# A row-wise cosine similarity on one core: all loads on one queue, tiles on another address grid, the last block in pieces, and most of the epilogue moved into the loop

## The chip, the cores and the metric

One core of a Trainium2 chip. The metric is the device time of one execution in microseconds (us). The kernel before takes 1268.29 us (median of 5 runs, 1268.15 to 1268.68). The profiled execution of it has a span of 1266.4 us; times in the traces count from its start.

## The reference

```python
# x, y: 8192 x 8192, float32
x_norm = np.linalg.norm(x, axis=1, keepdims=True)
y_norm = np.linalg.norm(y, axis=1, keepdims=True)
return np.sum(x * y, axis=1) / (x_norm.squeeze() * y_norm.squeeze() + 1e-8)
```

Each row needs three sums over 8192 columns: x·y, x·x and y·y. The inputs are 537 MB, the output is 32 KB.

## The kernel before

Rows are taken in 64 blocks of 128, one row in each partition. A block is a 4 MB tile of x and one of y, each 128 x 8192, with two buffers each. DVE (VectorE) multiplies x by y and sums; ACT (ScalarE) squares x and sums, then y. x is loaded through SP's DMA queue, y through ACT's.

```python
    consts = ctx.enter_context(tc.tile_pool(name="consts", bufs=1))
    xyacc = consts.tile([P, M], fp32)      # also xxacc, yyacc, ident: 1280 bytes in all
    # ... (cut)
    for b in range(nblk):
        # ... (cut; K is 1, so F is 8192 and there is one k)
            xt = xpool.tile([P, F], fp32)
            nc.sync.dma_start(out=xt, in_=x[r0 : r0 + P, c0 : c0 + F])
            yt = ypool.tile([P, F], fp32)
            nc.scalar.dma_start(out=yt, in_=y[r0 : r0 + P, c0 : c0 + F])
            prod = spool.tile([P, F], bf16, name="prod")
            nc.vector.tensor_tensor_reduce(out=prod, in0=xt, in1=yt, # ... (cut)
                accum_out=xyacc[:, m : m + 1])
            sqr = spool.tile([P, F], bf16, name="sqr")
            nc.scalar.activation(out=sqr, in_=xt, # Square (cut)
                accum_out=xxacc[:, m : m + 1])
            nc.scalar.activation(out=sqr, in_=yt, # Square (cut)
                accum_out=yyacc[:, m : m + 1])
    # epilogue, 64 columns, once at the end
    nc.vector.tensor_tensor(out=nn, in0=xxs, in1=yys, op=mult)
    nc.scalar.sqrt(out=sq, in_=nn)
    nc.vector.tensor_scalar(out=sqe, in0=sq, scalar1=1e-8, scalar2=None, op0=add)
    nc.vector.reciprocal(out=rcp, in_=sqe)
    nc.vector.tensor_tensor(out=res, in0=xys, in1=rcp, op=mult)
    # ... (cut: PSUM tile)
    nc.tensor.transpose(rest, res, ident)
    nc.vector.tensor_copy(out=ot, in_=rest)
    nc.sync.dma_start(out=out.rearrange("(b p) -> b p", p=P), in_=ot)
```

## Time and profile before

| stretch of the span, us | from | to | long |
|---|---|---|---|
| until the first input data moves | 0 | 1.8 | 1.8 |
| the input stream, to the last landing | 1.8 | 1248.4 | 1246.6 |
| to the end of ACT's last square and its sum | 1248.4 | 1260.1 | 11.8 |
| to the issue of the output store | 1260.1 | 1263.65 | 3.5 |
| to the end | 1263.65 | 1266.37 | 2.72 |

Begin with the question which engine is full. These are lines of the page of the kernel before: two digit rows and the DMA rows, each with 40 equal slices of the span (a digit is the busy share in tenths); then the shares of the chain that ended last, by line; then DVE's group of instructions (busy us, mean ns, idle us before them and what ended most of it).

```profile
span 1266.4 us, 830 instructions
...
DVE  2254453443543534535435345354353453543534
ACT  3777686686776866867768668677686686776776
...
DMA  9999999999999999999999999999999999999993
GB/s 409 436 431 431 431 431 431 431 431 431 432 434 436 431 435 432 431 431 431 431 431 431 431 433 434 434 431 436 431 432 431 431 431 431 431 433 431 437 431 146
...
DMA xt<-in_x_dram 42%; DMA yt<-in_y_dram 42%; DVE prod L55 14%; ACT sqr L72 1%; ACT sqr L66 0%; ACT L100 0%; DVEq L55 0%; DVE rcp L104 0%; SPq L50 0%; ACTq L52 0%; PE rest L111 0%; DVE xyacc L55 0%; ACTq L66 0%; DVE ot L113 0%; ACTq L140 0%
...
L55 DVE CUSTOM_DVE_ANT_0 prod<-xt,yt 128x8192 bf16<-128x8192 f32 x64 | 556.3, 8692 | 700.4 <-DMA yt<-in_y_dram 700.4
...
```

DVE and ACT have gaps in every slice; the DMA engines are at 9 tenths or more in 39 of 40 slices and move about 431 GB/s. DVE waits 700 us for y in all. The slices are coarse (they read 409 to 437 GB/s in the body); the period of a block, below, gives 431.8 GB/s. The last slice, at 146 GB/s, is the tail.

The chain of waits gives the period of a block. Columns: start, duration, what. This chain alternates between the loads of x and y, so it meets DVE once in three blocks.

```profile
...
1037.07 8.69 DVE prod L55
...
1045.83 25.07 DMA xt<-in_x_dram
...
1071.04 24.16 DMA yt<-in_y_dram
...
1095.35 8.69 DVE prod L55
...
1153.64 8.69 DVE prod L55
...
```

From 1037.07 to 1095.35 to 1153.64, three blocks take 58.28 and 58.29 us: 19.43 us a block, for 8.39 MB: 431.8 GB/s.

How long a load takes from issue to landing stands in the page's DMA issues (line, queue, count, KB each, median us):

```profile
...
yt<-in_y_dram ACTq DMA_DIRECT2D x64, 4096.0 KB, 24.2
xt<-in_x_dram SPq DMA_DIRECT2D x64, 4096.0 KB, 25.1
...
```

And the tail, in the timeline (start, duration, engine, line, operation; in brackets the idle time before it and who ended it):

```profile
...
1245.84 7.03 ACT L66 ACTIVATE sqr<-xt 128x8192 bf16<-128x8192 f32 x1 [5.13 <-DMA xt<-in_x_dram]
1248.53 8.69 DVE L55 CUSTOM_DVE_ANT_0 prod<-xt,yt 128x8192 bf16<-128x8192 f32 x1 [8.47 <-DMA yt<-in_y_dram]
...
1253.00 7.03 ACT L72 ACTIVATE sqr<-yt 128x8192 bf16<-128x8192 f32 x1
...
1259.94 0.19 ACT L72 ACTIVATION_READ_ACCUMULATOR sqr<-yt 128x1 f32 x1
1260.14 1.28 ACT L100 ACT_TABLE_LOAD   x1
...
1261.95 0.55 DVE L104 RECIPROCAL rcp<-sqe 128x64 f32<-128x64 f32 x1
...
1263.65 0.55 SPq L114 DMA_DIRECT2D out_dram<-ot  x1
```

The last x lands first and the last y 2.7 us later. ACT needs 14.3 us for both squares and starts only at 1245.84, so it, not DVE, ends the block. Then comes a second table load for Sqrt, of 1.28 us; the square root itself starts right behind it, at 1261.43.

### The profile page before, as it was taken

To read this page: it belongs to the slowest core of one execution; us is meant where nothing else is said; L and a number is where in the kernel's file an instruction comes from. 1 tells how busy PE (TensorE), PEld (TensorE's weight loads), DVE (VectorE), ACT (ScalarE), POOL (GpSimd) and SP (SyncE) were. 2 spreads that over 40 slices of the span, in tenths; PEclk is the share of its full clock that TensorE was granted. 3 is DMA by queue.
4 is the path that set the end of the run, shared out by engine and by line. 5 is a ranking of instruction groups with operands and counts; after the bars stand their busy time and mean duration, and the time that the engine had idled before them with its cause. 6 is when DMAs were issued, how large, how long until landed. Compare 5 with 4: busy or idle time off the path is not lost.

```text
span 1266.4 us, 830 instructions
## 1 busy us (share of the span) xinstructions
PE 0.4 (0%) x1; PEld 0.1 (0%) x1; DVE 558.3 (44%) x133; ACT 914.5 (72%) x259; POOL 0.7 (0%) x6
## 2 busy tenths in 40 slices
PE   0000000000000000000000000000000000000000
PEld 0000000000000000000000000000000000000000
DVE  2254453443543534535435345354353453543534
ACT  3777686686776866867768668677686686776776
POOL 0000000000000000000000000000000000000000
DMA  9999999999999999999999999999999999999993
GB/s 409 436 431 431 431 431 431 431 431 431 432 434 436 431 435 432 431 431 431 431 431 431 431 433 434 434 431 436 431 432 431 431 431 431 431 433 431 437 431 146
DMA packets 18519, 536.97 MB, mean 424 GB/s; under 512 B 2064, under 2 KB 2128, under 8 KB 2128
## 3 DMA queue, kind: packets, MB, share of 16 engines
q1 hardware_dynamic: 9296, 268.47, 49.3%
q10 hardware_dynamic: 9216, 268.44, 49.2%
q14 instruction: 7, 0.06, 0.0%
HBM read 536.87 MB, written 0.03 MB: 424 GB/s over the span
## 4 chain that ended last, share of the span: by engine, by line
DMA 83%; DVE 15%; ACT 1%; issue 1%; ACTq 0%; DVEq 0%; SPq 0%; PE 0%
DMA xt<-in_x_dram 42%; DMA yt<-in_y_dram 42%; DVE prod L55 14%; ACT sqr L72 1%; ACT sqr L66 0%; ACT L100 0%; DVEq L55 0%; DVE rcp L104 0%; SPq L50 0%; ACTq L52 0%; PE rest L111 0%; DVE xyacc L55 0%; ACTq L66 0%; DVE ot L113 0%; ACTq L140 0%
## 5 line engine op out<-in xcount | busy, mean ns | idle before, releaser
L55 DVE CUSTOM_DVE_ANT_0 prod<-xt,yt 128x8192 bf16<-128x8192 f32 x64 | 556.3, 8692 | 700.4 <-DMA yt<-in_y_dram 700.4
L66 ACT ACTIVATE sqr<-xt 128x8192 bf16<-128x8192 f32 x64 | 449.9, 7030 | 342.3 <-DMA xt<-in_x_dram 342.3
L72 ACT ACTIVATE sqr<-yt 128x8192 bf16<-128x8192 f32 x64 | 449.9, 7030 | 3.1 <-DMA yt<-in_y_dram 1.1
L66 ACT ACTIVATION_READ_ACCUMULATOR sqr<-xt 128x1 f32 x64 | 11.9, 187 | 0.0
L72 ACT ACTIVATION_READ_ACCUMULATOR sqr<-yt 128x1 f32 x64 | 11.9, 186 | 0.0
L55 DVE DVE_READ_ACCUMULATOR2_ANT xyacc<- 128x1 f32 x64 | 5.3, 82 | 0.0
L66 ACT ACT_TABLE_LOAD x1 | 1.3, 1283 | 1.7 <-PEq L129 1.7
L98 DVE TENSOR_TENSOR nn<-xxacc,yyacc 128x64 f32<-128x64 f32 x1 | 0.2, 226 | 2.9 <-ACT sqr L72 2.9
L100 ACT ACT_TABLE_LOAD x1 | 1.3, 1283 | 0.0
L102 DVE TENSOR_SCALAR sqe<-sq 128x64 f32<-128x64 f32 x1 | 0.2, 195 | 1.3 <-ACT sq L100 1.3
L111 PE MATMUL rest<-ident,res 128*64 128x128 f32 x1 | 0.4, 393 | 1262.9 <-DVE res L106 1262.9
L104 DVE RECIPROCAL rcp<-sqe 128x64 f32<-128x64 f32 x1 | 0.6, 554 | 0.0
L113 DVE COPY ot<-rest 64x128 f32<-64x128 f32 x1 | 0.3, 282 | 0.6 <-PE rest L111 0.6
masks.py:199 POOL TENSOR_SCALAR_AFFINE_SELECT ident<-ident 128x128 f32<-128x128 f32 x1 | 0.3, 295 | 0.1
L100 ACT ACTIVATE sq<-nn 128x64 f32<-128x64 f32 x1 | 0.3, 256 | 0.0
L111 PEld LDWEIGHTS rest<-ident,res 128*64 128x64 f32 x1 | 0.1, 128 | 1262.9 <-issue 1262.9
L106 DVE TENSOR_TENSOR res<-xyacc,rcp 128x64 f32<-128x64 f32 x1 | 0.2, 225 | 0.0
masks.py:197 POOL MEMSET ident<- 128x128 f32 x1 | 0.2, 205 | 0.3 <-POOLq L129 0.3
L129 POOL MEMSET const-bfloat16-1.0<- 128x1 bf16 x1 | 0.1, 103 | 0.0
L129 POOL MEMSET const-uint8-127<- 128x1 uint8 x1 | 0.1, 102 | 0.0
L129 POOL MEMSET const-float32-0.0<- 128x1 f32 x1 | 0.1, 100 | 0.2 <-issue 0.2
L129 POOL MEMSET const-float32-1.0<- 128x1 f32 x1 | 0.1, 100 | 0.0
## 6 DMA issues: line engine op xcount, KB each, us to landing
yt<-in_y_dram ACTq DMA_DIRECT2D x64, 4096.0 KB, 24.2
xt<-in_x_dram SPq DMA_DIRECT2D x64, 4096.0 KB, 25.1
out_dram<-ot SPq DMA_DIRECT2D x1, 32.0 KB, 1.9
```

What stands on the lines that cost most here:

```text
L55: nc.vector.tensor_tensor_reduce(out=prod, in0=xt, in1=yt, scale=1.0, scalar=0.0, op0=mult, op1=add, accum_out=xyacc[:, m : m + 1],)
L66: nc.scalar.activation(out=sqr, in_=xt, func=mybir.ActivationFunctionType.Square, accum_out=xxacc[:, m : m + 1],)
L72: nc.scalar.activation(out=sqr, in_=yt, func=mybir.ActivationFunctionType.Square, accum_out=yyacc[:, m : m + 1],)
L98: nc.vector.tensor_tensor(out=nn, in0=xxs, in1=yys, op=mult)
L100: nc.scalar.sqrt(out=sq, in_=nn)
L102: nc.vector.tensor_scalar(out=sqe, in0=sq, scalar1=1e-8, scalar2=None, op0=add)
L104: nc.vector.reciprocal(out=rcp, in_=sqe)
L106: nc.vector.tensor_tensor(out=res, in0=xys, in1=rcp, op=mult)
L111: nc.tensor.transpose(rest, res, ident)
L113: nc.vector.tensor_copy(out=ot, in_=rest)
L129: nc = _bacc.Bacc("TRN2", target_bir_lowering=False, num_devices=1)
```

## The change

It has four parts. All loads go to SP's queue. A padding tile moves x and y onto addresses that are multiples of 256 bytes (they were 128 bytes off: the first x tile stood at 17792 and now stands at 18176). The last block is loaded and reduced in pieces of 4096, 2048, 1024 and 1024 columns, so that little work is left after the last landing. And the epilogue of the first 62 blocks runs, and stores, beside the stream, with Sqrt's table set loaded at the start and used for Square as well; the add of 1e-8 is dropped. (The squares of x and of y also get a scratch tile each.) The core of the diff:

```diff
+    nl = nblk - 1
+    ne = nblk - 2
+    ends = [4096, 6144, 7168, 8192]
     # ... (cut: constants)
-    xyacc = consts.tile([P, M], fp32)
-    xxacc = consts.tile([P, M], fp32)
-    yyacc = consts.tile([P, M], fp32)
+    acc = consts.tile([P, 3 * nblk], fp32, name="acc")  # 768 bytes
+    fa = consts.tile([P, 3 * NP], fp32, name="fa")  # 48, takes 64
+    pad = consts.tile([P, 64], fp32, name="pad")  # rows of x and y on the 256-byte grid
     # ... (cut: the other tiles)
-            nc.sync.dma_start(out=xt, in_=x[r0 : r0 + P, c0 : c0 + F])
-            nc.scalar.dma_start(out=yt, in_=y[r0 : r0 + P, c0 : c0 + F])
+        if b < nl:
+            nc.sync.dma_start(out=xt, in_=x[r0 : r0 + P, :])
+            nc.sync.dma_start(out=yt, in_=y[r0 : r0 + P, :])
+            if b == 0:
+                nc.gpsimd.memset(one, 1.0)
+                nc.scalar.sqrt(out=dum, in_=one)  # loads the table set with Sqrt and Square
+                # ... (cut)
+            dve_dot(prod, xt, yt, a0v[:, 2, b : b + 1])
+            act_sq(sqx, xt, a0v[:, 0, b : b + 1])
+            act_sq(sqy, yt, a0v[:, 1, b : b + 1])
+            if b == ne - 1:  # the epilogue of the first 62 blocks
+                # ... (cut: mult, sqrt, reciprocal, mult on 62 columns)
+                nc.tensor.transpose(psE[0:ne, :], res[:, 0:ne], ident)
+                nc.vector.tensor_copy(out=ot[0:ne, :], in_=psE[0:ne, :])
+                nc.gpsimd.dma_start(out=outv[0:ne, :], in_=ot[0:ne, :])
+            continue
+        for k, (s, e) in enumerate(zip(starts, ends)):
+            cs = slice(s, e)
+            nc.sync.dma_start(out=xt[:, cs], in_=x[r0 : r0 + P, cs])
+            nc.sync.dma_start(out=yt[:, cs], in_=y[r0 : r0 + P, cs])
+            dve_dot(prod[:, cs], xt[:, cs], yt[:, cs], fav[:, 2, k : k + 1])
+            act_sq(sqx[:, cs], xt[:, cs], fav[:, 0, k : k + 1])
+            if k == 2:
+                dve_dot(sqy[:, cs], yt[:, cs], yt[:, cs], fav[:, 1, k : k + 1])
+            else:
+                act_sq(sqy[:, cs], yt[:, cs], fav[:, 1, k : k + 1])
+    # the last block's sums join its column; then the epilogue of the last two blocks
+    nc.vector.tensor_reduce(out=a0v[:, :, nl : nl + 1], in_=fav, axis=mybir.AxisListType.X, op=add)
+    nc.vector.tensor_tensor(out=nnL, in0=a0v[:, 0, ne:nblk], in1=a0v[:, 1, ne:nblk], op=mult)
+    nc.scalar.sqrt(out=sqL, in_=nnL)
     # ... (cut: reciprocal, mult, transpose, copy on 2 columns)
+    nc.sync.dma_start(out=outv[ne:nblk, :], in_=otL)
```

More of the change, by code (lines that the diff above doesn't have):

```diff
@@ L20 @@
     fp32 = mybir.dt.float32
+    bf16 = mybir.dt.bfloat16
     N, D = x.shape
@@ L25 @@
     F = D
-    K = D // F
-    M = nblk * K
-    bf16 = mybir.dt.bfloat16
     mult = mybir.AluOpType.mult
     add = mybir.AluOpType.add
+    nl = nblk - 1
+    ne = nblk - 2
+    sq_f = mybir.ActivationFunctionType.Square
+    ends = [4096, 6144, 7168, 8192]
+    starts = [0] + ends[:-1]
+    NP = len(ends)
     consts = ctx.enter_context(tc.tile_pool(name="consts", bufs=1))
-    xyacc = consts.tile([P, M], fp32)
-    xxacc = consts.tile([P, M], fp32)
-    yyacc = consts.tile([P, M], fp32)
+    acc = consts.tile([P, 3 * nblk], fp32, name="acc")
     ident = consts.tile([P, P], fp32)
-    make_identity(nc, ident)
+    fa = consts.tile([P, 3 * NP], fp32, name="fa")
+    one = consts.tile([P, 1], fp32, name="one")
+    dum = consts.tile([P, 1], fp32, name="dum")
+    pad = consts.tile([P, 64], fp32, name="pad")
+    a0v = acc.rearrange("p (g b) -> p g b", g=3)
+    fav = fa.rearrange("p (g k) -> p g k", g=3)
     xpool = ctx.enter_context(tc.tile_pool(name="xp", bufs=2))
@@ L42 @@
     spool = ctx.enter_context(tc.tile_pool(name="scratch", bufs=1))
+    fin = ctx.enter_context(tc.tile_pool(name="fin", bufs=1))
+    nn = fin.tile([P, nblk], fp32)
+    sq = fin.tile([P, nblk], fp32)
+    rcp = fin.tile([P, nblk], fp32)
+    res = fin.tile([P, nblk], fp32)
+    ot = fin.tile([nblk, P], fp32)
+    otL = fin.tile([2, P], fp32, name="otL")
+    nnL = fin.tile([P, 2], fp32, name="nnL")
+    sqL = fin.tile([P, 2], fp32, name="sqL")
+    rcpL = fin.tile([P, 2], fp32, name="rcpL")
@@ new lines, with dve_dot, act_sq @@
+    resL = fin.tile([P, 2], fp32, name="resL")
+    pspool = ctx.enter_context(tc.tile_pool(name="ps", bufs=1, space=bass.MemoryType.PSUM))
+    psE = pspool.tile([nblk, P], fp32, name="psE")
+    psL = pspool.tile([2, P], fp32, name="psL")
+    outv = out.rearrange("(b p) -> b p", p=P)
+    def dve_dot(o, a, b_, accum):
+        nc.vector.tensor_tensor_reduce(
+            out=o, in0=a, in1=b_, scale=1.0, scalar=0.0, op0=mult, op1=add, accum_out=accum
+        )
+    def act_sq(o, a, accum):
+        nc.scalar.activation(out=o, in_=a, func=sq_f, accum_out=accum)
@@ L44 @@
     for b in range(nblk):
         r0 = b * P
-        for k in range(K):
-            c0 = k * F
-            m = b * K + k
-            xt = xpool.tile([P, F], fp32)
-            nc.sync.dma_start(out=xt, in_=x[r0 : r0 + P, c0 : c0 + F])
-            yt = ypool.tile([P, F], fp32)
-            nc.scalar.dma_start(out=yt, in_=y[r0 : r0 + P, c0 : c0 + F])
-            prod = spool.tile([P, F], bf16, name="prod")
-            nc.vector.tensor_tensor_reduce(
-                out=prod,
-                in0=xt,
-                in1=yt,
-                scale=1.0,
-                scalar=0.0,
-                op0=mult,
-                op1=add,
-                accum_out=xyacc[:, m : m + 1],
-            )
-            sqr = spool.tile([P, F], bf16, name="sqr")
-            nc.scalar.activation(
-                out=sqr,
-                in_=xt,
-                func=mybir.ActivationFunctionType.Square,
-                accum_out=xxacc[:, m : m + 1],
-            )
-            nc.scalar.activation(
-                out=sqr,
-                in_=yt,
-                func=mybir.ActivationFunctionType.Square,
-                accum_out=yyacc[:, m : m + 1],
-            )
@@ L79 @@
-    fin = ctx.enter_context(tc.tile_pool(name="fin", bufs=1))
-    if K > 1:
-        ax = mybir.AxisListType.X
-        xys = fin.tile([P, nblk], fp32)
-        xxs = fin.tile([P, nblk], fp32)
-        yys = fin.tile([P, nblk], fp32)
-        nc.vector.tensor_reduce(
-            out=xys, in_=xyacc.rearrange("p (b k) -> p b k", k=K), axis=ax, op=add
-        )
-        nc.vector.tensor_reduce(
-            out=xxs, in_=xxacc.rearrange("p (b k) -> p b k", k=K), axis=ax, op=add
-        )
-        nc.vector.tensor_reduce(
-            out=yys, in_=yyacc.rearrange("p (b k) -> p b k", k=K), axis=ax, op=add
-        )
-    else:
-        xys, xxs, yys = xyacc, xxacc, yyacc
@@ L97 @@
-    nn = fin.tile([P, nblk], fp32)
-    nc.vector.tensor_tensor(out=nn, in0=xxs, in1=yys, op=mult)
-    sq = fin.tile([P, nblk], fp32)
-    nc.scalar.sqrt(out=sq, in_=nn)
-    sqe = fin.tile([P, nblk], fp32)
-    nc.vector.tensor_scalar(out=sqe, in0=sq, scalar1=1e-8, scalar2=None, op0=add)
-    rcp = fin.tile([P, nblk], fp32)
-    nc.vector.reciprocal(out=rcp, in_=sqe)
-    res = fin.tile([P, nblk], fp32)
-    nc.vector.tensor_tensor(out=res, in0=xys, in1=rcp, op=mult)
-    assert nblk <= P
-    pspool = ctx.enter_context(tc.tile_pool(name="ps", bufs=1, space=bass.MemoryType.PSUM))
@@ L110 @@
-    rest = pspool.tile([nblk, P], fp32, name="rest")
-    nc.tensor.transpose(rest, res, ident)
-    ot = fin.tile([nblk, P], fp32)
-    nc.vector.tensor_copy(out=ot, in_=rest)
-    nc.sync.dma_start(out=out.rearrange("(b p) -> b p", p=P), in_=ot)
+        xt = xpool.tile([P, F], fp32)
+        yt = ypool.tile([P, F], fp32)
+        prod = spool.tile([P, F], bf16, name="prod")
+        sqx = spool.tile([P, F], bf16, name="sqx")
+        sqy = spool.tile([P, F], bf16, name="sqy")
+        if b < nl:
[4 more added lines that the diff above has]
+                nc.scalar.sqrt(out=dum, in_=one)
+                nc.gpsimd.memset(pad, 0.0)
+                make_identity(nc, ident)
+            dve_dot(prod, xt, yt, a0v[:, 2, b : b + 1])
+            act_sq(sqx, xt, a0v[:, 0, b : b + 1])
+            act_sq(sqy, yt, a0v[:, 1, b : b + 1])
+            if b == ne - 1:
+                nc.vector.tensor_tensor(
+                    out=nn[:, 0:ne], in0=a0v[:, 0, 0:ne], in1=a0v[:, 1, 0:ne], op=mult
+                )
+                nc.scalar.sqrt(out=sq[:, 0:ne], in_=nn[:, 0:ne])
+                nc.vector.reciprocal(out=rcp[:, 0:ne], in_=sq[:, 0:ne])
+                nc.vector.tensor_tensor(
+                    out=res[:, 0:ne], in0=a0v[:, 2, 0:ne], in1=rcp[:, 0:ne], op=mult
+                )
+                nc.tensor.transpose(psE[0:ne, :], res[:, 0:ne], ident)
+                nc.vector.tensor_copy(out=ot[0:ne, :], in_=psE[0:ne, :])
+                nc.gpsimd.dma_start(out=outv[0:ne, :], in_=ot[0:ne, :])
+            continue
@@ new lines @@
+    nc.vector.tensor_reduce(out=a0v[:, :, nl : nl + 1], in_=fav, axis=mybir.AxisListType.X, op=add)
+    nc.vector.tensor_tensor(out=nnL, in0=a0v[:, 0, ne:nblk], in1=a0v[:, 1, ne:nblk], op=mult)
+    nc.scalar.sqrt(out=sqL, in_=nnL)
+    nc.vector.reciprocal(out=rcpL, in_=sqL)
+    nc.vector.tensor_tensor(out=resL, in0=a0v[:, 2, ne:nblk], in1=rcpL, op=mult)
+    nc.tensor.transpose(psL, resL, ident)
+    nc.vector.tensor_copy(out=otL, in_=psL)
+    nc.sync.dma_start(out=outv[ne:nblk, :], in_=otL)
```

## The prediction

> **What bounds the kernel now.** The input stream. The page's slices show the DMA engines at 9 tenths in 39 of 40 slices and about 431 GB/s; DVE is busy 44%, ACT 72%. In the chain of waits, one block (x and y, 8.39 MB) takes 19.43 us: three blocks per 58.29 us, 1153.6 to 1211.9. That is 431.7 GB/s. [...] The rest of the span is head and tail. By the timeline, the last y lands at 1248.5, and then 17.9 us carry no input: ACT squares x (begun 1245.8) and y, 8192 columns each, until 1260.1; table load 1.28; the 64-column chain to 1263.65; output store to 1266.4.
>
> **What the change does.**
> 1. Last block in pieces of 4096, 2048, 1024, 1024 columns, y's third square on DVE. ACT costs 7.03 us for 8192 columns, 0.26 for 64, plus 0.19 to read the sum, so I estimate 3.8, 2.1 and 1.3 us per piece. ACT is still busy with block 62's y when the pieces begin to land; laying the pieces out in time, ACT ends about 3.5 us after the last landing instead of 11.6. Saved: about 8 us.
> 2. Epilogue of blocks 0 to 61 moved under the stream (DVE waits 10.7 us in every block, so it is free). The last two blocks' epilogue works on 2 columns: no table load (Sqrt and Square share one set, loaded at the start), no add of 1e-8, reciprocal no longer 0.55 us; a small reduction (about 0.2 us) comes in. From ACT's end to the store about 1.8 us instead of 3.5. Saved: about 1.7 us. The store still costs its 2.7 us.
> 3. The x and y tiles move from SBUF addresses 128 bytes off the 256-byte grid (17792, read from the built program) onto it (18176). [...] This is the least certain term.
> 4. All loads on SP's queue instead of SP and ACT: the same engines, so no bandwidth. The queue is refilled with about 10 us of work still in it, so it should not run dry. Landing times should split: x about 20 us, y about 30 us, instead of 25 and 24. A separate scratch for sqy costs nothing.
>
> Nothing else in the body is on the critical path.
>
> **Predicted.** 1268.3 - 8 - 1.7 - 4 = 1254.5 us; range 1249 to 1260. Faster by over 2% (below 1242.9): 0.03; within 2%: 0.96; slower by over 2%: 0.01.
>
> **What would show each step.** (1) timeline: last landing to end of ACT's squares 3 to 4 us. (2) from there to the store's issue about 1.8 us, one table load in all. (3) block period 19.36 us or less; unchanged 19.43 means alignment is worth nothing. (4) median landings of 20 and 30 us, DMA slices without gaps.
>
> **What would make it wrong.** A bubble between transfers on a single queue, which the second queue hid: 0.1 us per transfer would be 13 us over 128. [...] The small 62-row store beside the stream delaying one DMA engine, so that the last piece lands late. ACT's backlog in the last block larger or smaller than laid out.

The sum came to 1254.5 us: 1268.3 less 8 (term 1), 1.7 (term 2) and 4 (term 3).

## The result, and the profile after

The kernel after takes 1251.64 us (median of 7 runs, 1251.49 to 1251.81), against 1268.33 us for the kernel before in the same rounds. The ratio is 0.9868, with a 95% interval of 0.9858 to 0.9878. Ratios here are the mean time of one kernel's fast runs over that of the other's of the same rounds, so not quite the ratio of the medians that are quoted. The results are correct.

| step, us in the two profiles | before | after | saved |
|---|---|---|---|
| start to the last landing of input | 1248.4 | 1244.4 | 4.0 |
| last landing to the end of ACT's last square | 11.8 | 1.8 | 10.0 |
| to the issue of the last store | 3.5 | 1.8 | 1.7 |
| issue of that store to the end | 2.72 | 2.07 | 0.7 |
| span | 1266.4 | 1250.0 | 16.4 |

The last landing is read from the trace's completion records: a load is taken as complete at the last of its 16 reports.

The lines of the page after that answer to those before:

```profile
span 1250.0 us, 929 instructions
...
DMA  9999999999999999999999999999999999999997
GB/s 403 436 436 433 428 431 436 436 435 430 428 435 436 434 435 428 430 436 436 434 434 429 430 436 435 436 431 429 433 436 435 436 428 428 436 436 436 433 428 318
...
DMA yt<-in_y_dram 75%; DVE prod L67 22%; ACT sqy L72 1%; SPq L82 1%; ACT sqx L72 1%; DVEq L67 0%; DVE acc L67 0%; SPq L83 0%; PE psL L121 0%; DVE otL L122 0%; ACT sqL L118 0%; DVE acc L116 0%; DVE rcpL L119 0%; DVE resL L120 0%; DVE nnL L117 0%
...
L86 ACT ACT_TABLE_LOAD x1 | 1.3, 1283 | 0.7 <-PEq L138 0.7
...
```

The last slice now carries 318 GB/s instead of 146: the tail is shorter. There is one table load, of 1283 ns; before there were two of that length. The chain now runs through y alone, since y, issued behind x in the same queue, is the later to land (29.4 us from issue against 20.1, below), and meets DVE once in two blocks:

```profile
...
836.75 8.69 DVE prod L67
...
845.93 29.38 DMA yt<-in_y_dram
...
875.47 8.69 DVE prod L67
...
914.19 8.69 DVE prod L67
...
```

From 836.75 to 875.47 to 914.19, two blocks take 38.72 us: 19.36 us a block instead of 19.43. The landing times split, x at 20.1 us and y, which stands behind it in the queue, at 29.4 us:

```profile
...
xt<-in_x_dram SPq DMA_DIRECT2D x63, 4096.0 KB, 20.1
yt<-in_y_dram SPq DMA_DIRECT2D x63, 4096.0 KB, 29.4
...
```

The tail of the timeline, from the store of the first 62 rows (POOL, 1216.18) on; ACT's and DVE's pieces of the last block between 1231.97 and 1245.03 are left out:

```profile
...
1216.18 0.67 POOL L103 DMA_DIRECT2D out_dram<-ot  x1 [1214.75 <-DVE ot L102]
...
1224.94 7.03 ACT L72 ACTIVATE sqy<-yt 128x8192 bf16<-128x8192 f32 x1 [2.62 <-DMA yt<-in_y_dram]
...
1231.97 3.60 ACT L72 ACTIVATE sqx<-xt 128x4096 bf16<-128x4096 f32 x1
...
1245.03 1.05 ACT L72 ACTIVATE sqy<-yt 128x1024 bf16<-128x1024 f32 x1
...
1245.97 0.19 ACT L72 ACTIVATION_READ_ACCUMULATOR sqy<-yt 128x1 f32 x1
1246.20 0.17 DVE L116 TENSOR_REDUCE acc<-fa 128x3 f32<-128x12 f32 x1 [0.45 <-ACT sqy L72]
...
1246.83 0.17 DVE L119 RECIPROCAL rcpL<-sqL 128x2 f32<-128x2 f32 x1 [0.27 <-ACT sqL L118]
...
1247.96 0.33 SPq L123 DMA_DIRECT2D out_dram<-otL  x1
```

Between 1224.94 and 1245.97 ACT is never idle: the pieces land faster than ACT squares them, and it ends 1.8 us after the last landing at 1244.4.

### The profile page after: what moved, and what is told of

Its sections match the earlier page's. It is cut to its first block, busy times and chain, and to the rows that moved or that the text cites. A ratio compares the mean times of both kernels' runs of the same rounds, so it can differ in the third digit from the quotient of the medians.

```text
span 1250.0 us, 929 instructions
## 1 busy us (share of the span) xinstructions
PE 0.8 (0%) x2; PEld 0.2 (0%) x2; DVE 560.5 (45%) x145; ACT 913.5 (73%) x270; POOL 1.5 (0%) x9
## 4 chain that ended last, share of the span: by engine, by line
DMA 75%; DVE 22%; ACT 1%; SPq 1%; issue 1%; DVEq 0%; PE 0%; ACTq 0%
DMA yt<-in_y_dram 75%; DVE prod L67 22%; ACT sqy L72 1%; SPq L82 1%; ACT sqx L72 1%; DVEq L67 0%; DVE acc L67 0%; SPq L83 0%; PE psL L121 0%; DVE otL L122 0%; ACT sqL L118 0%; DVE acc L116 0%; DVE rcpL L119 0%; DVE resL L120 0%; DVE nnL L117 0%
## 5 line engine op out<-in xcount | busy, mean ns | idle before, releaser
L67 DVE CUSTOM_DVE_ANT_0 prod<-xt,yt 128x8192 bf16<-128x8192 f32 (+2 forms) x67 | 556.8, 8310 | 685.2 <-DMA yt<-in_y_dram 685.1
L72 ACT ACTIVATE sqx<-xt 128x8192 bf16<-128x8192 f32 (+2 forms) x67 | 450.4, 6723 | 168.6 <-DMA xt<-in_x_dram 168.6
L72 ACT ACTIVATE sqy<-yt 128x8192 bf16<-128x8192 f32 (+1 forms) x66 | 449.4, 6810 | 161.7 <-DMA yt<-in_y_dram 161.7
L72 ACT ACTIVATION_READ_ACCUMULATOR sqx<-xt 128x1 f32 x67 | 12.5, 187 | 0.0
L72 ACT ACTIVATION_READ_ACCUMULATOR sqy<-yt 128x1 f32 x66 | 12.3, 187 | 0.0
L67 DVE DVE_READ_ACCUMULATOR2_ANT acc<- 128x1 f32 x63 | 5.2, 82 | 0.0
L86 ACT ACT_TABLE_LOAD x1 | 1.3, 1283 | 0.7 <-PEq L138 0.7
L101 PEld LDWEIGHTS psE<-ident,res 128*62 128x62 f32 x1 | 0.1, 129 | 1215.1 <-issue 1215.1
## 6 DMA issues: line engine op xcount, KB each, us to landing
xt<-in_x_dram SPq DMA_DIRECT2D x63, 4096.0 KB, 20.1
yt<-in_y_dram SPq DMA_DIRECT2D x63, 4096.0 KB, 29.4
```

What stands on the lines that cost most here:

```text
L67: nc.vector.tensor_tensor_reduce(out=o, in0=a, in1=b_, scale=1.0, scalar=0.0, op0=mult, op1=add, accum_out=accum)
L72: nc.scalar.activation(out=o, in_=a, func=sq_f, accum_out=accum)
L86: nc.scalar.sqrt(out=dum, in_=one) # loads the table set with Sqrt and Square
L101: nc.tensor.transpose(psE[0:ne, :], res[:, 0:ne], ident)
```

## The experiments

The prediction was near the measured time. But a sum can be near with wrong terms, and one part of the change (the queue) had been given no value at all. So each part was undone alone in the kernel after, and the two that touch the stream were also done alone in the kernel before.

### Address grid and queue: four corners

Theory A: the stream's 4 us come from the addresses. Theory Q: they come from the single queue. The trace records each DMA packet; a 32 KB packet is one row of one tile, and there are 16384 of them (16128 where the last block is in pieces). Their mean duration measures the stream without the tail.

`b_grid` is the kernel before on the grid:

```diff
     make_identity(nc, ident)
+    pad = consts.tile([P, 32], fp32, name="pad")  # 128 bytes: x and y on the 256-byte grid
+    nc.gpsimd.memset(pad, 0.0)
```

> The kernel before with 128 bytes of padding, so that x and y tiles start on the 256-byte grid; still two queues, tail untouched. Theory A (the offset costs the stream): the mean DMA record of a 32 KB row falls from 1217.6 ns to 1213.7 ns as in the kernel after, the period of a block from 19.42 to 19.36 us, the time by 4 us to 1264.3. Theory Q (two queues cost the stream, the address nothing): rows stay at 1217.6 ns and the time at 1268.3.

`b_one` is the kernel before on one queue:

```diff
-            nc.scalar.dma_start(out=yt, in_=y[r0 : r0 + P, c0 : c0 + F])
+            nc.sync.dma_start(out=yt, in_=y[r0 : r0 + P, c0 : c0 + F])
```

> The kernel before with y's loads moved to SP's queue; tiles still 128 bytes off the grid, tail untouched. Theory A: rows stay near 1217.6 ns; the time stays at 1268.3 or moves by at most about 1 us (the last y lands at nearly the same time, but x earlier, which lets ACT square x before y lands: the tail alone may gain 3 to 4 us, from ACT's 7 us for x ending before the last landing; that is not the stream). Theory Q: rows at 1213.7 ns, and 4 us more off the time.

`a_off` is the kernel after off the grid by 128 bytes:

```diff
-    pad = consts.tile([P, 64], fp32, name="pad")
+    pad = consts.tile([P, 32], fp32, name="pad")
```

> The kernel after with 128 bytes less padding, so that x and y tiles are again 128 bytes off the grid; one queue, all else as after. Theory A: rows back at 1217.6 ns, block period 19.42 us, time 1255.6 (+4). Theory Q: 1213.7 ns and 1251.6.

`a_two` is the kernel after on two queues:

```diff
         if b < nl:
             nc.sync.dma_start(out=xt, in_=x[r0 : r0 + P, :])
-            nc.sync.dma_start(out=yt, in_=y[r0 : r0 + P, :])
+            nc.scalar.dma_start(out=yt, in_=y[r0 : r0 + P, :])
```

> The kernel after with y's loads of the first 63 blocks back on ACT's queue; tiles on the grid, the last block's pieces still on SP. Theory A: rows stay at 1213.7 ns and the time within 1 us of 1251.6, but for what the order of landing does at the end. Theory Q: rows at 1217.6 ns, time 1255.6. Landings of x and y about 25 and 24 us again under both.

Measured, with rounds of its own in which the kernel before took 1268.17 us:

| kernel | grid | queues | mean 32 KB packet, ns | time, us | ratio to before |
|---|---|---|---|---|---|
| before | 128 off | 2 | 1217.6 | 1268.17 | 1 |
| b_grid | on | 2 | 1213.6 | 1263.73 | 0.9965 (0.9953 to 0.9978) |
| b_one | 128 off | 1 | 1217.6 | 1263.99 | 0.9968 (0.9955 to 0.9980) |
| a_off | 128 off | 1 | 1217.7 | 1255.98 | 0.9904 (0.9890 to 0.9917) |
| a_two | on | 2 | 1213.8 | 1254.04 | 0.9889 (0.9874 to 0.9904) |
| after | on | 1 | 1213.7 | 1251.64 (other rounds) | 0.9868 |

The packets follow the address and not the queue, in all four corners: theory A holds and Q falls. The arithmetic closes: 16384 packets over 16 engines are 1024 for each in the mean, and 1024 x 4.0 ns is 4.1 us; the two grid comparisons give 4.4 and 4.3 us. (Over all rounds the kernel before took 1268.17 to 1268.40 us, so times of different rounds can be compared to about 0.2 us.)

Still, the single queue is worth 4.2 us alone in the kernel before and 2.4 us in the kernel after, without a faster packet. It acts in the tail, by the order in which the last loads land. `b_one`, timeline of its tail:

```profile
...
1238.63 7.03 ACT L66 ACTIVATE sqr<-xt 128x8192 bf16<-128x8192 f32 x1 [2.64 <-DMA xt<-in_x_dram]
...
1248.32 7.03 ACT L72 ACTIVATE sqr<-yt 128x8192 bf16<-128x8192 f32 x1 [2.57 <-DMA yt<-in_y_dram]
1248.41 8.69 DVE L55 CUSTOM_DVE_ANT_0 prod<-xt,yt 128x8192 bf16<-128x8192 f32 x1 [10.76 <-DMA yt<-in_y_dram]
...
1255.46 1.28 ACT L100 ACT_TABLE_LOAD   x1
1257.03 0.08 DVE L55 DVE_READ_ACCUMULATOR2_ANT xyacc<- 128x1 f32 x1
...
1259.49 0.55 SPq L114 DMA_DIRECT2D out_dram<-ot  x1
```

The last y lands when it did before (1248.2 against 1248.4). But x landed 9.7 us ahead of it, at 1238.6, so ACT has x squared before y comes and ends at 1255.5 instead of 1260.1. What ends the block is now DVE with its 8.69 us, at 1257.1: 3.0 us earlier than ACT did before. The other 1.1 us of the gain is the second table load, which now runs while DVE still works: from the end of the block to the issue of the store it is 2.4 us instead of 3.5. In `a_two` the same acts one block earlier. Its timeline:

```profile
...
1227.21 7.03 ACT L72 ACTIVATE sqy<-yt 128x8192 bf16<-128x8192 f32 x1 [1.41 <-DMA yt<-in_y_dram]
...
1234.24 3.60 ACT L72 ACTIVATE sqx<-xt 128x4096 bf16<-128x4096 f32 x1
...
1248.25 0.18 ACT L72 ACTIVATION_READ_ACCUMULATOR sqy<-yt 128x1 f32 x1
...
```

Against the kernel after, y of block 62 starts to be squared at 1227.21 instead of 1224.94, since with two queues it lands that much later; ACT then has no gap, and ends 2.3 us later, though the last input lands at almost the same time (1244.5 against 1244.4).

One point of the expectation for `a_two` failed: its median landings were 18.9 us for x and 16.8 us for y, not 25 and 24. No run asked why, or whether the time depends on it.

### The pieces alone undone

`a_whole` (with the padding corrected by 32 bytes, since `fa` shrinks, so that the tiles stay on the grid):

```diff
-    ends = [4096, 6144, 7168, 8192]
+    ends = [8192]
-            if k == 2:
+            if k == 99:
```

> The kernel after with the last block loaded and reduced whole (one piece); grid, one queue and early epilogue kept. If the pieces are worth what the prediction's first term says they are worth by themselves (8 us), 1259.6. My theory now: with one queue x of the last block lands 10 us before y, so ACT is no longer the limit and DVE's 8.69 us after the last landing is; ACT ended 1.8 us after the last landing in the kernel after, so the pieces are worth about 8.8 - 1.8 - 0.4 (small rows cost 0.4 us of stream) = 6.6 us: 1258.2. The rest of the tail's gain came from the queue.

The 0.4 us for small rows are an estimate from the trace after: its packets of 16, 8 and 4 KB took 611, 309 and 159 ns in the mean, 4, 6 and 7 ns over their share of the 1213.7 ns of a 32 KB row, and the mean share of one of 16 engines is 16, 16 and 32 of them.

It took 1258.67 us (before in these rounds: 1268.26 us; ratio 0.9924, 0.9911 to 0.9936). That is 7.0 us above the kernel after. Its timeline:

```profile
...
1234.44 7.03 ACT L72 ACTIVATE sqx<-xt 128x8192 bf16<-128x8192 f32 x1 [2.54 <-DMA xt<-in_x_dram]
...
1244.09 7.03 ACT L72 ACTIVATE sqy<-yt 128x8192 bf16<-128x8192 f32 x1 [2.53 <-DMA yt<-in_y_dram]
1244.17 8.69 DVE L67 CUSTOM_DVE_ANT_0 prod<-xt,yt 128x8192 bf16<-128x8192 f32 x1 [10.64 <-DMA yt<-in_y_dram]
...
1252.97 0.16 DVE L116 TENSOR_REDUCE acc<-fa 128x3 f32<-128x3 f32 x1
...
```

With one queue, ACT has squared x before y lands (the start at 1234.44 leaves 2.5 us of rest), and DVE's 8.69 us from 1244.17 end the block. So the pieces do not take 11.8 us of ACT to 1.8 by themselves. The queue takes ACT out of the way, and the pieces then cut DVE's one long instruction: DVE ended 8.9 us after the last landing here (1244.0 to 1252.9), and the block in the kernel after ends 1.8 us after it. With two queues the pieces cut ACT's work instead: ACT ends 11.9 us after the last landing in `b_grid` (1243.8 to 1255.7) and 4.0 us after it in `a_two` (1244.5 to 1248.4), though these two also differ in the epilogue, and all of the last block in `a_two` comes through one queue.

### The early epilogue undone, and the store beside the stream

`a_epi` puts the whole 64-column epilogue, the second table load, the add of 1e-8 and a single store back at the end:

```diff
-                nc.scalar.sqrt(out=dum, in_=one)  # loads the table set with Sqrt and Square
-            if b == ne - 1:  # the epilogue of the first 62 blocks
-                # ... (cut: all of it)
     nc.vector.tensor_reduce(out=a0v[:, :, nl : nl + 1], in_=fav, axis=mybir.AxisListType.X, op=add)
-    # ... (cut: the 2-column epilogue)
+    nc.vector.tensor_tensor(out=nn, in0=a0v[:, 0, :], in1=a0v[:, 1, :], op=mult)
+    nc.scalar.sqrt(out=sq, in_=nn)
+    nc.vector.tensor_scalar(out=sq, in0=sq, scalar1=1e-8, scalar2=None, op0=add)
+    # ... (cut: reciprocal, mult, transpose, copy)
+    nc.sync.dma_start(out=outv, in_=ot)
```

> The kernel after with the whole epilogue (64 columns, table load for Sqrt, the add of 1e-8, one store of 64 rows) at the end again, nothing stored beside the stream. Theory: ACT's end to the store's issue 1.76 us becomes about 3.6 (0.2 reduction + the 3.5 us of before), the store 2.07 becomes 2.75: 1254.1 to 1254.3. If the store beside the stream had cost the stream anything that counts, it would be up to 0.5 us less than this.

It took 1253.80 us (ratio 0.9885, 0.9870 to 0.9900): 2.2 us above the kernel after, a little under the range expected. From ACT's end to the issue of the store it was 3.5 us in the profile, and the store took 2.74 us. Against that, ACT ended 0.26 us earlier than in the kernel after (1245.90 against 1246.16).

`a_late` keeps the early arithmetic and takes only the store beside the stream away:

```diff
-                nc.tensor.transpose(psE[0:ne, :], res[:, 0:ne], ident)
-                nc.vector.tensor_copy(out=ot[0:ne, :], in_=psE[0:ne, :])
-                nc.gpsimd.dma_start(out=outv[0:ne, :], in_=ot[0:ne, :])
     # ... (cut)
-    nc.tensor.transpose(psL, resL, ident)
-    nc.vector.tensor_copy(out=otL, in_=psL)
-    nc.sync.dma_start(out=outv[ne:nblk, :], in_=otL)
+    nc.tensor.transpose(psE, res, ident)
+    nc.vector.tensor_copy(out=ot, in_=psE)
+    nc.sync.dma_start(out=outv, in_=ot)
```

> The kernel after without the store of 62 rows beside the stream: one transposition, copy and store of all 64 rows at the end; the rest of the early epilogue kept. The landings of block 61 and after spread from 1.62 to 2.15 us where that store ran; theory B (the store delays one DMA engine): the spread stays near 1.6 and the last landing comes 0.4 to 0.5 us earlier. The time: theory C (ACT's backlog of squares, not the landing, ends the last block) gives no gain from that, and the 64-row store costs 0.7 us: 1252.3. If the landing ends the block: 1251.8.

It took 1252.29 us (ratio 0.9874, 0.9860 to 0.9887), the figure of theory C; but the profile shows that C was right for the wrong reason. Without the store, the 16 reports of the last load spread over 1.66 us instead of 2.02, and the last landing came at 1244.04 instead of 1244.38, which looks like theory B. But in the kernel after the spread had already grown, from 1.62 to 2.15 us, in a load that had landed by 1215.12, and the store was only issued at 1216.18. The DMA records show something else just before: a packet of queue 14, which the page calls "instruction" (8 KB, 309 ns, at 1208.98), and behind it one 32 KB row that took 1751 ns instead of 1213. `a_late` has the same pair (at 1209.91, a row of 1746 ns), but there the spread stayed at 1.7 us. The first reports of the last load came at 1242.4 in both. So the difference is no work of the store, and theory B falls: by its size (the spread grew by 0.53 us), the row's 0.54 us fell on the part of the load that reported last already in the kernel after, and not in `a_late`; that is inferred, since the records name no engine. The earlier landing did reach ACT's end, which came 0.35 us earlier, because block 62's y landed earlier too (ACT starts on it at 1224.59 instead of 1224.94), and that is where ACT's unbroken run of squares starts. The gain was then more than paid back: 0.7 us for a store of 64 rows instead of 2 (2.72 against 2.07 us from issue to end) and 0.1 us for the wider transposition. So storing early saves about 0.8 us at the end by the profiles, and 0.65 us by the timed runs; a cost of the store to the stream was not seen.

### Is ACT's backlog the last limit?

`a_best` loads block 62 in two halves as well and the last block in six pieces, so that both engines are further ahead when the last pieces land:

```diff
-    ends = [4096, 6144, 7168, 8192]
+    cut = {nl - 1: [4096, 8192], nl: [2048, 4096, 6144, 7168, 7680, 8192]}
     # ... (cut: one fa for each of the two blocks, padding kept on the grid)
-            if k == 2:
+            if k == 3:
```

> The kernel after with block 62 in two halves and the last block in six pieces (2048, 2048, 2048, 1024, 512, 512), so that ACT and DVE have half of block 62 behind them when its last half lands. Theory C: ACT's end comes 0.9 to 1.2 us after the last landing instead of 1.8; minus about 0.2 us of stream for more small rows: 1250.7 to 1251.1. If ACT's backlog was not the limit: 1251.6 or more.

It took 1251.58 us (ratio 0.9868, 0.9854 to 0.9881; the kernel after has 0.9868): no gain that can be told from noise. The timeline of its end:

```profile
...
1244.93 0.69 DVE L65 CUSTOM_DVE_ANT_0 prod<-xt,yt 128x512 bf16<-128x512 f32 x1
1245.01 0.19 ACT L70 ACTIVATION_READ_ACCUMULATOR sqy<-yt 128x1 f32 x1
...
1245.73 0.17 DVE L114 TENSOR_REDUCE acc<-fa 128x3 f32<-128x18 f32 x1
...
1247.50 0.32 SPq L121 DMA_DIRECT2D out_dram<-otL  x1
```

ACT did end earlier, at 1245.2, 0.75 us after the last landing (1244.45). But now DVE's last products end the block, at about 1245.6, and the store is issued 0.46 us earlier than in the kernel after (1247.50 against 1247.96). The span is 0.3 us shorter, which the timed runs do not confirm. The part of theory C that the backlog is ACT's holds for the kernel after. The expectation that taking it away gains 0.5 to 0.9 us was wrong, because DVE is only half a microsecond behind. No version tried here beats the kernel after by an amount that these runs can show.

### What does a row off the grid pay for?

At 128 bytes off the grid a row takes about 4 ns longer (1217.6 or 1217.7 ns against 1213.6 to 1213.8). How the price depends on the offset was open. Theory W: it grows in proportion to the offset, so that 64, 128 and 192 bytes would cost about 2, 4 and 6 ns a row. Theory X: it is one fixed price. `a_off64` and `a_off192` are the kernel after with `pad` of 16 and 48 columns:

```diff
-    pad = consts.tile([P, 64], fp32, name="pad")
+    pad = consts.tile([P, 16], fp32, name="pad")   # a_off192: [P, 48]
```

> The kernel after with the x and y tiles 64 bytes off the 256-byte grid instead of on it. Theory W [...]: rows of about 1215.6 ns, half of the 3.9 ns that 128 bytes cost; time about 1253.8. Theory X (a row off the grid pays a fixed price[...]): 1217.6 ns and 1256.0 as at 128 bytes.

> The kernel after with the x and y tiles 192 bytes off the grid. Theory W: [...]rows of about 1219.5 ns, time about 1258.1. Theory X: 1217.6 ns and 1256.0.

| offset, bytes | mean 32 KB packet, ns | time, us | ratio to before |
|---|---|---|---|
| 0 (after) | 1213.7 | 1251.64 | 0.9868 |
| 64 | 1217.6 | 1256.01 | 0.9902 (0.9886 to 0.9919) |
| 128 (a_off) | 1217.7 | 1255.98 | 0.9904 (0.9890 to 0.9917) |
| 192 | 1217.6 | 1255.94 | 0.9902 (0.9887 to 0.9917) |

In the mean theory X holds, and W falls: about 3.9 ns a row at every offset tried (1217.6, 1217.7 and 1217.6 ns against 1213.7). But it is not one fixed price for each row. On the grid 99.7% of the 32 KB records take 1213 ns. At 128 bytes off, 20% still do, 30% take 1218 and 17% take 1221; at 64 and at 192 bytes off, 9 to 10% take 1213, 46 to 47% take 1215 and 18 to 19% take 1222. What inside the DMA engine makes this difference was not shown.

## Why the prediction was right, point by point

- **The bound and its consequence.** "The input stream" was right, and with it that nothing in the body but the stream's own rate could move (a block went from 19.43 to 19.36 us). The whole gain lies in the tail (12.4 us of span) and in the rate (4.0 us). The sum was 2.9 us too high; 2.0 of that is term 1 and about 0.6 the store of term 2.
- **Term 1, the last block ("Saved: about 8 us").** Right in mechanism, too small: 10.0 us. "ACT ends about 3.5 us after the last landing" was the mis-sized step; it measured 1.8. ACT's run of squares after block 62's y landed took 21.2 us (1224.94 to 1246.16). My estimates per piece, 3.8, 2.1 and 1.3 us, had added a full 0.19 us read to each, 15.7 us for ACT's seven squares of the last block; the trace has 14.2 (1231.97 to 1246.16), since the next square starts before the read has ended (for instance 1231.88 plus 0.19 against 1231.97). That is 1.5 of the 1.7 us.
- **Term 2, the epilogue ("about 1.7 us").** 3.5 us became 1.8: right. One table load, of 1283 ns, served every square on ACT and both square roots; the reciprocal on 2 columns took 0.17 us and the small reduction 0.17. "The store still costs its 2.7 us" was wrong by 0.6: a store of 2 rows took 2.07 us. Undone as a whole, with all its side effects, this part is worth 2.2 us.
- **Term 3, the grid (4 us in the sum, called the least certain).** Right: 4.3 to 4.4 us by two pairs of kernels, packets of 1217.6 ns against 1213.7 on one queue and on two. The size was a guess that happened to fit: what it was derived from is shown by no trace or run here. The mean price of a row was the same at all three offsets.
- **Term 4, the queue ("the same engines, so no bandwidth").** True for bandwidth (packets of 1213.6 ns with two queues, 1213.7 with one), and the landing times were 20.1 and 29.4 us as predicted. At 9.68 us a load, half a block, the 20.1 us put about 10 us of work before x in the queue (an estimate from these two figures), as the prediction has it. That the separate scratch for sqy costs nothing was not tested. But the sum gave the queue no worth of its own, and it has one: 4.2 us alone in the kernel before, 2.4 us in the kernel after. It came in unnamed through the end of ACT that term 1 forecasts, which lies 4.0 us after the last landing in `a_two` and 1.8 in the kernel after. Whether the layout behind term 1 had x land ahead of y is not in the text.
- **What could have gone wrong.** A bubble between transfers on one queue did not appear: packets of 1213.7 ns on one queue against 1213.6 and 1213.8 on two, and the last input landed at 1248.2 us in `b_one` (one queue) against 1248.4 in the kernel before. Nor was the small store seen to delay a DMA engine: the spread of landings that seemed to show it had grown before the store was issued.

Undone one at a time in the kernel after, the parts cost 4.3 (grid), 2.4 (queue), 7.0 (pieces) and 2.2 us (early epilogue), 15.9 in all, of 16.7 us. They need not add up: the queue is worth less where the pieces are and where no table load is left to hide, and the pieces shorten DVE's end with one queue and ACT's with two. The splitting of the remaining 0.8 us was not pursued. One more thing the traces show: the 16 reports of a load spread further apart over the run, from about 0.4 us between the first and the last of them to about 2 us at the end (2.4 before, 2.0 after). In the kernel after, up to the store of 62 rows, each step of more than 0.1 us comes in the load that lands next after a packet of queue 14, "instruction": packets at 210.6, 385.0, 414.3, 1004.0, 1034.6 and 1209.0 us, loads landed at 216.5, 390.9, 420.4, 1011.1, 1040.5 and 1215.1. Behind each of its seven such packets one 32 KB row took 1455 to 1751 ns instead of 1213. No run changed the number of these packets.

## What to carry to other kernels

When a kernel sits at the rate of its input stream, ask what is still to be done once the last byte has landed. Lay that out for every engine, because shortening one engine's remainder only helps down to the next one's: in the kernel before ACT was last, with ACT out of the way DVE was, and in the kernel after the two end within half a microsecond of each other. The queue that a load is issued on changes no bandwidth here (packets of 1213.6 and 1213.7 ns), but it changes the order of landing, and at the end of this stream that order was worth 4.2 us in the kernel before and 2.4 us in the kernel after. Look at where the allocator has put the tiles: a start 64, 128 or 192 bytes off the 256-byte grid cost about 0.3% of a row's time in the mean here (1217.6 or 1217.7 ns against 1213.7).
